# A decoder layer on one core: residual projection by tile, loads in program order, and a closing stage for one pair of experts

## The chip, the cores and the metric

The kernel runs on one core of one Trainium2 chip. A core has TensorE (PE), which multiplies matrices into an accumulator memory (PSUM) of eight banks, VectorE (DVE), ScalarE (ACT), GpSimd (POOL) and SyncE (SP), the engine that issues nearly all of this kernel's loads. Each engine works through its own list of instructions in order. An instruction that has to wait for another engine or for a DMA holds up all that is behind it on its own list. The metric is the device time of one execution in microseconds. The kernel before takes 1101.13 us (median of 3 runs, 1100.86 to 1102.59).

## The reference

One decoder layer on 512 tokens of width 1024, all in float32. The mixer's inner work is left out here; it is not touched.

```
y = hybrid_mixer(x, ...)                       # ends in a product with w_out (1024 x 1024)
x = layer_norm(DN_ALPHA * x + y, ln1_g, ln1_b)
y = memory_cross_attention(x, mem, x_wq, x_wkv, x_wo)
x = layer_norm(DN_ALPHA * x + y, ln2_g, ln2_b)
y = hier_moe(x, ...)
x = layer_norm(DN_ALPHA * x + y, ln3_g, ln3_b)

def memory_cross_attention(x, mem, wq, wkv, wo):   # 4 heads of 128, 256 memory tokens
    q = x @ wq;  k, v = split(mem @ wkv)
    p = softmax(q k^T / sqrt(128))
    return (p v) @ wo

def hier_moe(...):     # each token: the best of 4 groups, then the 2 best of its 8 experts
    gu = xc @ w_gu[e]                              # 1024 x 1024, e of 32 experts
    return (silu(gu[:, :512]) * gu[:, 512:]) @ w_down[e]   # 512 x 1024, times the token's weight, summed per token
```

## The kernel before, in words

The kernel has three stretches: the mixer, `mid` (L952 on: the residual projection with the first norm, then cross-attention with the second norm), and `moe` (L1894 on).

**Residual projection (L978 to L991).** The 512 tokens are four tiles q of 128 rows (`xt[q]`). The product of the mixer's output with `wout` is made in two halves ch of 512 columns. A half has four chunks kk of weights. Each chunk is loaded (`raw`, L220), split into a high and a low part (`wh` on ACT, L231, and `wl` on DVE, L232), and multiplied with all four tiles, so the four accumulators of a half are done at about the same time. `residual` (L878) then adds them to `xt[q]`. When the second half is in, the first norm of each tile follows (its square sum on ACT, the two passes of `norm_apply` on DVE), then eight transposes of the tile on PE (L1032) and their splits into `XH` and `XL` (L224, L225).

**Cross-attention.** K comes from `wk` and the memory (PSUM tile `s`, split into `kh` and `kl`), V from `wxv`. `project(f)` makes the queries of head f from `wq`. `score(f)` makes two PSUM tiles of scores (each half's row maximum on DVE, L1086, its product with -scale on DVE, L1087), the exponentials on ACT (L1092) and the division on DVE. `turn(f)` transposes the probabilities on PE and copies them to `PT` (the first half on ACT, L1111). `attend(f)` multiplies `PT` with V, `widen(k)` splits a chunk of `wxo`, and `out` multiplies with it.

**Experts.** The 32 experts are worked through in 16 pairs, p = 0 to 15. The weights of a pair are 12 units of 1 MB: 8 of the gate and up matrices (`gu`) and 4 of the down matrix (`dn`). Units are loaded in a fixed order into a ring of 24 homes (the ring proper and memory of earlier stages, so names such as `XL`, `raw` or `xt` stand for homes too). `load_first` (L1623) issues the first 24. `eat` (L1641) issues the next load into a home whose unit has been used. A pair takes eight steps `hidden(k)` into the two accumulators `pg`, then `activate` (SiLU on ACT, a product on DVE), `turn` (four transposes and a copy to `hT`), four `down_quarter` calls of 256 columns each, `scaled` (times the token's weight, split into `yh` and `yl`), and `combine`, which multiplies with the one-hot matrix `ohT` to add the pair's rows to the tokens, while the next pair's hidden steps run. The last two pairs are closed together by `finish` (L1724 to L1837): pair 14 stops after its transposes (L2005 to L2007). `finish` then mixes pair 15's hidden steps with the eight down quarters of both pairs, their scalings and eight products with `ohT` ("spills", L1746), four for each pair, and the third norm by 256 columns each, to write the last two tiles as four half rows (`ship`, L1708, with `idx2`). The last 16 loads stand in an order of their own (L1632, L1633). Tiles 0 and 1 have been written earlier (`settle`).

**What sets the order.** A list scheduler orders the instructions of the mixer and of `mid` up to L1051. From there all engines but SP keep the order in which the code is written. SP's list is ordered by the scheduler up to L1936 in `moe`, and only from there by the program.

Of the kernel before, what the change touches and what calls it, by code (L numbers as in the profile page):

```python
# [23 lines left out]
D = 1024  # L24
# [176 lines left out]
class K:  # L201
# [750 lines left out]
    def mid(self, outer, order):  # L952
# [13 lines left out]
        with ExitStack() as st:  # L966
# [12 lines left out]
            with ExitStack() as sw:  # L979
                pre = self.pool(sw, "pre", side="right")  # L980
                for ch in range(2):
                    acc = [self.t(ps, [128, 512], F32, "acc", 4) for _ in range(NT)]
                    for kk in range(4):
                        j = 4 * ch + kk
                        h, l = self.wsplit(a["wout"][j], wp=pre if 3 <= j < 7 else None)
                        for q in range(NT):
                            tk = slice(128 * q, 128 * q + 128)
                            self.mm3(acc[q], [(XH[:, 2 * kk + i, tk], XL[:, 2 * kk + i, tk], h[:, 512 * i:512 * i + 512],
                                               l[:, 512 * i:512 * i + 512]) for i in range(2)], start=kk == 0, stop=kk == 3)
                    for q in range(NT):  # L990
                        self.residual(stat[q], q, ch, acc[q], ALPHA)  # L991
# [57 lines left out]
            scale = 128.0 ** -0.5  # L1049
            ws = [self.wsplit(a["wq"][f]) for f in range(2)]  # L1050
# [22 lines left out]

            def score(f):
                qh, ql = qs[f]
                sm = self.t(mp, [128, 3, 4], F32, "sm", 2)
                tiles = []
                sps = []
                for b in range(2):
# [7 lines left out]
                    nc.vector.tensor_scalar(sm[:, 1, cs], sm[:, 0, cs], -scale, None, op0=ALU.mult)  # L1087
# [84 lines left out]
            score(3)  # L1172
            turn(2)
            widen(3, True)
# [133 lines left out]
    def route_init(self, mq, tri):  # L1308
# [17 lines left out]
        self.idx2 = self.t(rp, [128, NT, 2], I32, "idx2")  # L1326
# [47 lines left out]
    def use_records(self, mp, p, ps):  # L1374
# [18 lines left out]
        for i in range(2):  # L1393
            nc.vector.tensor_scalar(self.idx2[:, :, i], rec[:, :, 6], 2.0, float(i), op0=ALU.mult, op1=ALU.add)
# [228 lines left out]
    def load_first(self):  # L1623
# [36 lines left out]
    def activate(self, mp, pg, h=None):  # L1660
        if h is None:
            h, hT = self.halves(mp)
        else:
            hT = [self.t(self.m0, [128, 256], F32, f"oh{i}", 1) for i in range(2)]
        with self.tc.high_priority():
            self.nc.scalar.activation(h, pg[0], AF.Silu)  # L1666
            self.nc.vector.tensor_tensor(h, h, pg[1], op=ALU.mult)  # L1667
        return h, hT

    def turn(self, ps, h, hT):  # L1670
        pt = self.t(ps, [128, 512], F32, "t", 2)
        with self.tc.high_priority():
            for k in range(4):
                self.nc.tensor.transpose(pt[:, 128 * k:128 * k + 128], h[:, 128 * k:128 * k + 128], self.ident)  # L1674
            if isinstance(hT, list):
                for i, t in enumerate(hT):
                    self.nc.scalar.activation(t, pt[:, 256 * i:256 * i + 256], AF.Copy)
            else:
                self.nc.scalar.activation(hT, pt, AF.Copy)  # L1679
# [8 lines left out]
    def down_quarter(self, py, hT, p, c, experts, ks=range(4)):  # L1688
        us = [12 * p + 8 + 2 * (c // 2) + i for i in range(2)]
        for k in ks:  # L1690
            for i in experts:
                t = hT[k // 2][:, 128 * (k % 2):] if isinstance(hT, list) else hT[:, 128 * k:]
                self.mm(py[c][64 * i:64 * i + 64], t[:, 64 * i:64 * i + 64],
                        self.got[us[i]][c % 2][:, 256 * k:256 * k + 256], k == 0, k == 3)
        if k == 3 and c % 2:
# [12 lines left out]
    def ship(self, q, h=None):  # L1708
        o = self.views.pop()
        if h is None:  # L1710
            ix, z = self.idx[:, q:q + 1], self.xt[q]
        else:
            ix, o, z = self.idx2[:, q, h:h + 1], o.rearrange("t (h c) -> (t h) c", h=2), self.xt[q][:, 512 * h:512 * h + 512]
# [10 lines left out]
    def finish(self, mp, ps, last, hidden, turn):  # L1724
# [8 lines left out]
        def down(b, j, *experts, ks=range(4)):  # L1733
            if (b, j) not in py:
                py[b, j] = self.t(ps, [128, 512], F32, "ts"[j], 2)[:, :256]
            self.down_quarter({b: py[b, j]}, last[j][1], last[j][0], b, experts, ks)

        def scale(b, j):
            ws, o = last[j][3], y[b % 2][:, j]
            nc.scalar.activation(o[:, 0], py[b, j], AF.Copy, scale=ws)  # L1740
            nc.vector.scalar_tensor_tensor(o[:, 1], py[b, j], ws, f32(o[:, 0]), op0=ALU.mult, op1=ALU.subtract)

        def spill(b, j):
            for n, q in enumerate(span):
                if j == 0 and n == 0:
                    t = self.t(ps, [128, 512], F32, "acc", 4)  # L1746
                    acc[b, q], acc[b, q + 1] = t[:, :256], t[:, 256:]
                for i in range(2):
                    self.mm(acc[b, q], last[j][2][:, 128 * q:128 * q + 128], y[b % 2][:, j, i], j == 0 and i == 0 and n == 0, j == 1 and i == 1)

        def add(b):
            for q in span:
                z = self.xt[q][:, 256 * b:256 * b + 256]
                nc.vector.scalar_tensor_tensor(z, z, 1.0, acc[b, q], op0=ALU.mult, op1=ALU.add, accum_out=c(b, q))

        def square(b, qs=span):
            for q in qs:
# [9 lines left out]
        for k in range(4):  # L1767
            hidden(k)
        down(0, 0, 0, 1)
        scale(0, 0)  # L1770
        for k in range(4, NK):
            hidden(k)
        last.append(turn(lambda: spill(0, 0)))
        down(0, 1, 0, 1)
        scale(0, 1)
        down(1, 0, 0, 1)
        scale(1, 0)
        spill(0, 1)
        add(0)
        nc.vector.tensor_scalar(v(4), v(0), -4.0 / D ** 1.5, None, op0=ALU.mult)  # L1780
        down(1, 1, 0)
        spill(1, 0)
        down(1, 1, 1)
        scale(1, 1)
        square(0)
        down(2, 0, 0, 1)
        scale(2, 0)
        spill(1, 1)
        add(1)
        tt(9, 0, 1, ALU.add)  # L1790
        down(3, 0, 0, 1)
        scale(3, 0)
        spill(2, 0)
        square(1)
        down(2, 1, 0)
        spill(3, 0)
        down(2, 1, 1)
        scale(2, 1)
        down(3, 1, 0, 1, ks=(0, 1))
        spill(2, 1)  # L1800
        add(2)
        square(2)
        down(3, 1, 0, 1, ks=(2, 3))
        scale(3, 1)
# [4 lines left out]
        spill(3, 1)  # L1809
        add(3)  # L1810
        square(3)
        tt(5, 5, 7, ALU.add)
        stt(10, 3, -1.0 / D, 10, ALU.mult, ALU.add)
        stt(9, 3, -1.0 / D, 9, ALU.mult, ALU.add)
        stt(10, 10, -1.0, 10, ALU.mult, ALU.mult)
        halves = [(q, h) for q in span for h in range(2)]
        gb = self.gb3

        def centre(q, h):
            cs = slice(512 * h, 512 * h + 512)  # L1820
            z = self.xt[q][:, cs]
# [220 lines left out]
```

## Time and profile before

| | |
|---|---|
| median of 3 runs | 1101.13 us |
| profiled execution | 1106.79 us, of which the span of the instructions is 1105.2 us |
| TensorE | busy 1049.9 us, 95% of the span |
| VectorE / ScalarE / GpSimd | 49% / 37% / 11% |
| mean granted TensorE clock | 0.974 of full speed |
| moved by DMA | 266.61 MB, mean 241 GB/s over the span |

The second part of the page shows the span in 40 slices. The rate of the DMA is between 40 and 245 GB/s in the first half of the span and 413 to 421 GB/s in most slices from the 26th on, while PE is busy nine tenths of nearly every slice. A busy PE need not be one that computes at its full rate. A stretch table (windows) gives for a stretch each engine's busy time, the granted clock (1.00 is the full one), and the share of time in which the core's 16 DMA engines are busy.

### The profile page before, as it was taken

What the parts mean: (1) busy time and instruction counts of PE and PEld (TensorE: products, weight loads), DVE (VectorE), ACT (ScalarE), POOL (GpSimd) and SP (SyncE); (2) the same over time, 40 slices, a digit from 0 to 9 for tenths busy, and PEclk for the clock granted to TensorE, in tenths of its full rate; (3) what the DMA queues carried; (4) which work ended last, traced back from release to release, by engine and by line L of the source; (5) the groups of instructions that cost most, each with busy time, mean ns of one, the idle gap of its engine ahead of it and who ended that gap; (6) DMA issues with size and microseconds to landing.
All of it is one profiled execution on the core that took longest, in us unless ns stands there. A gap on an engine that the chain in (4) does not pass through costs nothing. (4 is left out here: it accounts for less than half of the span.)

```text
span 1105.2 us, 14593 instructions
## 1 busy us (share of the span) xinstructions
PE 1049.9 (95%) x5645; PEld 716.4 (65%) x5645; DVE 537.4 (49%) x1194; ACT 408.3 (37%) x763; POOL 117.0 (11%) x124
## 2 busy tenths in 40 slices
PE   7999999999999999998899999999999999999884
PEld 5688777778788778787768655465644565555342
DVE  6436656879956533646457444324341334322314
ACT  6325656557544422524356312031202122212112
POOL 1000002301311112326030000000000000000001
PEclk9999999999999999998999989999998999999987
DMA  6612123112322122666366879989999999999981
GB/s 244 233 63 77 58 70 120 40 58 96 105 77 79 55 95 82 245 241 236 126 235 240 334 304 386 413 360 414 419 420 403 394 421 419 419 421 419 419 371 39
DMA packets 52186, 266.61 MB, mean 241 GB/s; under 512 B 5905, under 2 KB 6193, under 8 KB 31505
## 3 DMA queue, kind: packets, MB, share of 16 engines
q1 hardware_dynamic: 49104, 255.18, 59.2%
q0 software_dynamic: 2432, 8.36, 2.0%
q10 hardware_dynamic: 576, 2.10, 0.6%
q8 instruction: 46, 0.75, 0.3%
q14 instruction: 28, 0.22, 0.1%
HBM read 261.42 MB, written 4.19 MB: 240 GB/s over the span
## 5 line engine op out<-in xcount | busy, mean ns | idle before, releaser
L240 PE MATMUL acc<-ring,xg 128*64 128x512 f32 x776 | 188.7, 600 | 7.1 <-DMA ring<-gu 6.3
L240 PEld LDWEIGHTS acc<-ring,xg 128*64 128x64 f32 x776 | 60.8, 138 | 107.2 <-issue 99.4
L232 DVE TENSOR_TENSOR wl<-raw,wh 128x1024 fp32r<-128x1024 f32 x63 | 78.1, 1242 | 79.1 <-PE mm L240 41.7
L240 PE MATMUL mm<-XH,wh 128*128 128x512 f32 x392 | 105.9, 399 | 6.6 <-ACT XH L224 5.1
L231 ACT ACTIVATE wh<-raw 128x1024 fp32r<-128x1024 f32 x71 | 75.1, 1059 | 94.3 <-PE mm L240 57.2
L240 PE MATMUL mm<-XL,wh 128*128 128x512 f32 x392 | 106.5, 397 | 0.0
L240 PE MATMUL mm<-XH,wl 128*128 128x512 f32 x392 | 105.9, 396 | 0.0
L240 PEld LDWEIGHTS mm<-XH,wh 128*128 128x128 f32 x392 | 73.0, 189 | 24.3 <-ACT XH L224 5.1
L240 PEld LDWEIGHTS mm<-XH,wl 128*128 128x128 f32 x392 | 73.3, 189 | 18.7 <-issue 3.8
L240 PEld LDWEIGHTS mm<-XL,wh 128*128 128x128 f32 x392 | 72.9, 189 | 15.9 <-issue 1.2
L1666 ACT ACTIVATE hh<-acc 128x512 f32<-128x512 f32 x15 | 9.0, 598 | 195.0 <-PE acc L240 182.1
L240 PE MATMUL t<-ring,hh 128*64 128x256 f32 x640 | 79.9, 381 | 0.7 <-ACT hh L1679 0.7
L1667 DVE TENSOR_TENSOR hh<-hh,acc 128x512 f32<-128x512 f32 x15 | 10.3, 688 | 139.6 <-PE acc L240 139.6
L1705 DVE SCALAR_TENSOR_TENSOR yl<-t,ws,yh 128x512 fp32r<-128x512 f32 x28 | 20.8, 750 | 107.6 <-ACT yh L1704 107.6
L240 PEld LDWEIGHTS t<-ring,hh 128*64 128x64 f32 x640 | 49.7, 137 | 23.5 <-ACT hh L1679 2.4
L856 POOL TENSOR_TENSOR mix<-mix,gate 128x512 f32<-128x512 f32 x24 | 37.6, 1571 | 191.2 <-DVE gate L855 173.5
L1565 ACT ACTIVATE xg<-acc,gbt 128x128 f32<-128x128 f32 x128 | 45.8, 477 | 21.8 <-PE acc L240 21.8
L240 PE MATMUL acc<-XL,xg 128*64 128x512 f32 x112 | 52.6, 620 | 1.2 <-DMA XL<-gu 1.2
L240 PE MATMUL s<-in,in 128*128 128x256 f32 (+5 forms) x198 | 43.8, 342 | 0.7 <-ACT S L630 0.7
L1704 ACT ACTIVATE yh<-t,ws 128x512 fp32r<-128x512 f32 x28 | 19.0, 687 | 66.8 <-PE t L240 52.4
L559 ACT ACTIVATE S<-S,sm 128x128 f32<-128x128 f32 (+3 forms) x48 | 26.7, 556 | 39.1 <-DVE sm L557 38.8
L240 PEld LDWEIGHTS s<-in,in 128*128 128x128 f32 (+1 forms) x198 | 33.3, 189 | 8.1 <-ACT S L630 0.9
(502 smaller groups left out, 1897.6 us busy)
## 6 DMA issues: line engine op xcount, KB each, us to landing
ring<-gu SPq DMA_DIRECT2D x95, 1024.0 KB, 13.5
ring<-dn SPq DMA_DIRECT2D x40, 1024.0 KB, 15.0
raw<-wing SPq DMA_DIRECT2D x32, 512.0 KB, 3.6
XL<-gu SPq DMA_DIRECT2D x14, 1024.0 KB, 12.5
ring<-gu SPq DMA_DIRECT2D x18, 512.0 KB, 13.0
XL<-dn SPq DMA_DIRECT2D x8, 1024.0 KB, 14.4
raw<-winf SPq DMA_DIRECT2D x15, 512.0 KB, 3.7
raw<-gu SPq DMA_DIRECT2D x13, 512.0 KB, 9.8
```

The source lines that it names most:

```text
L231: self.nc.scalar.activation(h, r, AF.Copy)
L232: (self.nc.gpsimd if pool else self.nc.vector).tensor_tensor(l, r, f32(h), op=ALU.subtract)
L240: self.nc.tensor.matmul(out, lhsT, rhs, start=start, stop=stop, skip_group_check=True)
L559: nc.scalar.activation(s[:, :n], s[:, :n], AF.Exp, bias=sm[:, 0, q:q + 1], scale=-1.0, accum_out=sm[:, 1, q:q + 1])
L856: nc.gpsimd.tensor_tensor(mix[d], mix[d], g, op=ALU.add)
L1565: self.nc.scalar.activation(t[:, d, :], p[:, d - 2 * b, w * k:w * k + w], AF.Identity, scale=self.gbt[:, d:d + 1], bias=self.gbt[:, NK + d ...
L1666: self.nc.scalar.activation(h, pg[0], AF.Silu)
L1667: self.nc.vector.tensor_tensor(h, h, pg[1], op=ALU.mult)
L1704: nc.scalar.activation(yh[:, cs], py[ch], AF.Copy, scale=ws)
L1705: nc.vector.scalar_tensor_tensor(yl[:, cs], py[ch], ws, f32(yh[:, cs]), op0=ALU.mult, op1=ALU.subtract)
```

## The change

1. **Residual projection by tile.** The second half of the columns has all its four chunks of weights split first and is then multiplied tile by tile; each tile's residual follows its own product.
2. **SP's list in program order from the loads of `wq` on.** The `manual_schedule` for SP is opened ahead of the first `wq` load in `mid` and no longer at `load_first`.
3. **Scores.** The product with -scale (L1087) becomes a Copy with a scale on ACT. For head 3, `score` is taken apart: its products, then `turn(2)` with its copy, then its exponentials.
4. **The last two pairs.** Pair 14 is closed as every other pair is, with its `combine` beside the hidden steps of pair 15 (two more `next(work)` at k = 3 and 5). `finish` closes pair 15 alone: four down quarters, four spills. The last 16 loads are in plain order. The last two tiles are written as two whole rows; `idx2` and its two DVE instructions go.

```diff
@@ mid
-                for ch in range(2):
-                    acc = [self.t(ps, [128, 512], F32, "acc", 4) for _ in range(NT)]
-                    for kk in range(4):
-                        j = 4 * ch + kk
-                        h, l = self.wsplit(a["wout"][j], wp=pre if 3 <= j < 7 else None)
-                        for q in range(NT):
...
-                    for q in range(NT):
-                        self.residual(stat[q], q, ch, acc[q], ALPHA)
...
+                w = [chunk(4 + kk) for kk in range(4)]
+                for q in range(NT):
+                    acc = self.t(ps, [128, 512], F32, "acc", 4)
                     for kk in range(4):
+                        product(acc, w[kk], kk, q)
+                    self.residual(stat[q], q, 1, acc, ALPHA)
...
             scale = 128.0 ** -0.5
+            order.enter_context(self.tc.manual_schedule(engines={nc.sync.engine}))
             ws = [self.wsplit(a["wq"][f]) for f in range(2)]
             order.enter_context(self.tc.manual_schedule(engines=self.engines))
@@ score
-                    nc.vector.tensor_scalar(sm[:, 1, cs], sm[:, 0, cs], -scale, None, op0=ALU.mult)
+                    nc.scalar.activation(sm[:, 1, cs], sm[:, 0, cs], AF.Copy, scale=-scale)
...
-            score(3)
+            products(3)
             turn(2)
+            soften(3)
@@ load_first
-        span = lambda x, y: list(range(n - x, n - y))
-        order = list(range(n - 16)) + span(12, 8) + span(16, 14) + span(8, 4) + span(4, 2) + span(14, 12) + span(2, 0)
-        self.in_ring = [j for j in order if j not in self.once and j not in self.again.values()]
+        self.in_ring = [j for j in range(n) if j not in self.once and j not in self.again.values()]
@@ moe
-        loads = ExitStack()
-        loads.enter_context(self.tc.manual_schedule(engines={nc.sync.engine}))
         self.load_first()
...
+                if p == n - 1 and k in (3, 5):
+                    next(work)
+                    next(work)
...
+            if p == n - 1:
+                self.finish(mp, ps, hT, p, ohT, ws)
+                break
...
-            if p == n - 2:
-                last, done = [(p, hT, ohT, ws)], None
-                continue
@@ finish (new order of its steps)
+        down(0)
+        scale(0)
+        down(1)
+        scale(1)
+        spill(0)
         add(0)
...
         square(0)
+        down(2)
+        spill(1)
+        scale(2)
         add(1)
+        square(1)
...
+        spill(2)
+        down(3)
         add(2)
+        scale(3)
         square(2)
...
+        spill(3)
         add(3)
         square(3)
...
         nc.gpsimd.tensor_tensor(v(11), v(5), self.mhalf.to_broadcast([128, 2]), op=ALU.pow)
+        centre(span[0], 1)
+        centre(span[1], 0)
+        for h in range(2):
+            apply(span[0], h)
+        self.ship(span[0])
+        centre(span[1], 1)
+        for h in range(2):
+            apply(span[1], h)
+        self.ship(span[1])
```

How the lists of the engines change at three places follows, first before, then now. A row is a line of the code, the operation, out<-in with the buffers' numbers, and the shape of what is moved or multiplied; x2 means two in a row.

PE in the second half of the residual projection, before: `acc_3978` to `acc_3981` are the accumulators of tiles 0 to 3, `wh_4044` the third chunk of weights.

```order
L240 MATMUL acc_3978<-wh_4044,XH_3780 128x512 x2
L240 MATMUL acc_3978<-wl_4045,XH_3780 128x512 x2
L240 MATMUL acc_3978<-wh_4044,XL_3781 128x512 x2
L240 MATMUL acc_3979<-wh_4044,XH_3780 128x512 x2
L240 MATMUL acc_3979<-wl_4045,XH_3780 128x512 x2
L240 MATMUL acc_3979<-wh_4044,XL_3781 128x512 x2
L240 MATMUL acc_3980<-wh_4044,XH_3780 128x512 x2
L240 MATMUL acc_3980<-wl_4045,XH_3780 128x512 x2
L240 MATMUL acc_3980<-wh_4044,XL_3781 128x512 x2
```

The same place now: `acc_4080` is tile 3's accumulator, `wh_3980` to `wh_3992` are chunks, and `xt_788` is tile 0.

```order
L240 MATMUL acc_4080<-wh_3980,XH_3780 128x512 x2
L240 MATMUL acc_4080<-wl_3981,XH_3780 128x512 x2
L240 MATMUL acc_4080<-wh_3980,XL_3781 128x512 x2
L240 MATMUL acc_4080<-wh_3986,XH_3780 128x512 x2
L240 MATMUL acc_4080<-wl_3987,XH_3780 128x512 x2
L240 MATMUL acc_4080<-wh_3986,XL_3781 128x512
L1042 MATMUL t_4346<-ident_58,xt_788_3805 128x128 x4
L1042 MATMUL t_4353<-ident_58,xt_788_3805 128x128 x4
L240 MATMUL acc_4080<-wh_3986,XL_3781 128x512
L240 MATMUL acc_4080<-wh_3992,XH_3780 128x512 x2
L240 MATMUL acc_4080<-wl_3993,XH_3780 128x512 x2
L240 MATMUL acc_4080<-wh_3992,XL_3781 128x512 x2
```

Before, each chunk went through all tiles and no tile was done until the last chunk. Now tile 3 takes its chunks one after another at the end, and the eight transposes of tile 0, whose norm lies behind its own product, stand amid tile 3's product.

SP ahead of the stream of expert weights, before: four loads into the ring stand ahead of these rows, and the other two `wq` and the `wxo` loads behind.

```order
L220 DMA raw_4261<-wxv 128x1024
L220 DMA raw_4279<-wxv 128x1024
L220 DMA raw_4297<-wxv 128x1024
L220 DMA raw_4315<-wxv 128x1024
L1609 DMA ring_1064_5332<-gu 128x2048
L1609 DMA ring_1065_5333<-gu 128x2048
L1609 DMA ring_1066_5334<-gu 128x2048
L1615 DMA ring_1063_5331<-gu 128x1024
L1615 DMA ring_4893<-gu 128x1024
L220 DMA raw_4484<-wq 128x1024
```

SP now, from the last `wxv` load on.

```order
L220 DMA raw_4315<-wxv 128x1024
L220 DMA raw_4485<-wq 128x1024
L220 DMA raw_4491<-wq 128x1024
L220 DMA raw_4526<-wq 128x1024
L220 DMA raw_4561<-wq 128x1024
L220 DMA raw_4626<-wxo 128x1024
L220 DMA raw_4628<-wxo 128x1024
L220 DMA raw_4630<-wxo 128x1024
L220 DMA raw_4681<-wxo 128x1024
L1628 DMA ring_1058_5328<-gu 128x2048
L1628 DMA ring_1059_5329<-gu 128x2048
```

The eight 1 MB units that stood among the loads of cross-attention (seven whole rows `ring<-gu` and one in two halves) now stand behind its last `wxo` load, and the `wq` loads stand right behind `wxv`.

SP at the end of the stream, before, from the first `gu` unit of pair 15 on (a unit is a row of 128x2048 or two of 128x1024; `dn` here is pair 14's).

```order
L1609 DMA ring_1065_5333<-gu 128x2048
L1609 DMA ring_1066_5334<-gu 128x2048
L1615 DMA ring_1063_5331<-gu 128x1024
L1615 DMA ring_4893<-gu 128x1024
L1609 DMA XL_4719<-gu 128x2048
L1609 DMA XL_4719<-dn 128x2048
L1615 DMA raw_4894<-dn 128x1024
L1615 DMA raw_4895<-dn 128x1024
L1609 DMA ring_1067_5335<-gu 128x2048
L1609 DMA ring_1068_5336<-gu 128x2048
```

The same places now.

```order
L1628 DMA ring_1064_5334<-dn 128x2048
L1628 DMA ring_1065_5335<-dn 128x2048
L1634 DMA ring_1062_5332<-dn 128x1024
L1634 DMA ring_4894<-dn 128x1024
L1628 DMA XL_4720<-dn 128x2048
L1628 DMA XL_4720<-gu 128x2048
L1634 DMA raw_4895<-gu 128x1024
L1634 DMA raw_4896<-gu 128x1024
L1628 DMA ring_1066_5336<-gu 128x2048
L1628 DMA ring_1067_5337<-gu 128x2048
```

Before, pair 15's `gu` units come first with two of pair 14's `dn` units between them, and pair 14's last two `dn` units come behind, among pair 15's. Now pair 14's four `dn` units come first, and pair 15's eight `gu` units follow.

## Rows read from the trace of the kernel before

**Rows 1.** The page: the span; busy time, share and instructions of TensorE.

```profile
span 1105.2 us, 14593 instructions
PE 1049.9 (95%) x5645; PEld 716.4 (65%) x5645; DVE 537.4 (49%) x1194; ACT 408.3 (37%) x763; POOL 117.0 (11%) x124
```

**Rows 2.** Stretches (start:end, length, busy us of PE, PEld, DVE, ACT, POOL, clock, DMA share, GB/s).

```profile
557.00:611.60 54.60, 51.45 (x291) 42.24 (x290) 38.60 (x158) 29.82 (x61) 11.69 (x12) 0.97 0.67 250
611.60:740.00 128.40, 123.34 (x777) 70.86 (x778) 46.09 (x132) 33.34 (x73) 3.94 (x4) 0.96 0.91 363
740.00:1074.50 334.50, 318.98 (x1912) 166.09 (x1908) 110.01 (x249) 65.14 (x142) 4.92 (x6) 0.98 1.01 415
1057.20:1066.60 9.40, 9.40 (x33) 2.71 (x33) 0.00 (x0) 0.60 (x1) 0.00 (x0) 0.74 1.01 420
```

**Rows 3.** Waits of SP, 620 to 740 us (total us, times, longest us).

```profile
SPq L1609 <- PE t L240: 38.0, 8, 14.2
```

**Rows 4.** Waits of PE, 500 to 531 us.

```profile
PE s L240 <- DVE kl L225: 3.9, 1, 3.9
PE acc L240 <- ACT wh L231: 3.0, 1, 3.0
PE t L1032 <- DVE XL L225: 1.1, 1, 1.1
```

**Rows 5.** Timeline of SP around cross-attention (start, duration, [idle before <-releaser]).

```profile
473.12 15.72 SPq L1609 DMA_DIRECT2D ring<-gu  x4
...
516.54 14.93 SPq L220 DMA_DIRECT2D raw<-wq  x4
...
558.08 0.38 SPq L220 DMA_DIRECT2D raw<-wxo  x1
```

**Rows 6.** Timeline of PE, then of ACT, around the K, V and query products.

```profile
500.60 1.11 PE L240 MATMUL s<-ol,wh 128*128 128x256 f32 x8
...
508.80 2.08 PE L240 MATMUL s<-oh,wh 128*128 128x256 f32 x8 [3.89 <-DVE kl L225]
...
529.91 3.52 PE L240 MATMUL acc<-XH,wh 128*128 128x512 f32 x8 [3.00 <-ACT wh L231]
...
535.12 1.98 PE L240 MATMUL acc<-XH,wl 128*128 128x512 f32 x8
...
528.80 2.17 ACT L231 ACTIVATE wh<-raw 128x1024 fp32r<-128x1024 f32 x2 [1.45 <-DMA raw<-wq]
```

**Rows 7.** Tile `xt` on DVE, 480 to 531 us (ns min/median/max); a row of POOL's timeline.

```profile
L915 DVE SCALAR_TENSOR_TENSOR xt<-xt,stat,ln x8: 737/744/2891, 491.3 to 507.7; 128x512 f32<-128x512 f32 x8
...
508.13 2.51 POOL L232 TENSOR_TENSOR wl<-raw,wh 128x1024 fp32r<-128x1024 f32 x1
```

**Rows 8.** Timeline, all engines, at the scores; then ACT at 622 us.

```profile
568.52 1.68 DVE L1087 TENSOR_SCALAR sm<-sm 128x2 f32<-128x2 f32 x1
...
571.86 1.12 PE L240 MATMUL acc<-PT,vm 128*128 128x512 f32 x2 [2.25 <-ACT PT L1111]
...
622.69 0.30 ACT L1480 ACTIVATE wsc<-wsc 128x4 f32<-128x4 f32 x1
```

**Rows 9.** Timeline of PE, the last two pairs.

```profile
1036.20 3.65 PE L240 MATMUL acc<-ring,xg 128*64 128x512 f32 x16 [1.52 <-DMA ring<-gu]
...
1057.14 9.51 PE L240 MATMUL acc<-ring,xg 128*64 128x512 f32 x32 [4.29 <-DMA ring<-gu]
...
1068.65 1.95 PE L240 MATMUL s<-ring,oh 128*64 128x256 f32 x16 [0.47 <-ACT oh L1677]
...
1072.25 0.74 PE L240 MATMUL acc<-yh,ohT 128*128 128x256 f32 x4
...
1090.52 1.14 PE L240 MATMUL acc<-yl,ohT 128*128 128x256 f32 x4 [1.05 <-ACT yl L1740]
```

**Rows 10.** Timeline of DVE, then of POOL, behind the last product.

```profile
1095.76 2.73 DVE L1827 SCALAR_TENSOR_TENSOR xt<-xt,stat,wl 128x512 f32<-128x512 f32 x4
...
1100.96 0.97 POOL L1714 DMA_INDIRECT out<-xt,idx  x1 [0.30 <-issue]
```

More of the change, by code (lines that the diff above doesn't have):

```diff
@@ L1072, in mid, with products @@
             probs = {}
+            raws = {}
             def score(f):
+                products(f)
+                soften(f)
+            def products(f):
                 qh, ql = qs[f]
                 sm = self.t(mp, [128, 3, 4], F32, "sm", 2)
-                tiles = []
                 sps = []
@@ L1658, in hidden, with activate @@
             self.eat(*us)
[L1660 to L1664, printed above, removed]
+    def activate(self, mp, pg):
+        h, hT = self.halves(mp)
         with self.tc.high_priority():
@@ L1674, in turn @@
                 self.nc.tensor.transpose(pt[:, 128 * k:128 * k + 128], h[:, 128 * k:128 * k + 128], self.ident)
[L1675 to L1679, printed above, removed]
+            self.nc.scalar.activation(hT, pt, AF.Copy)
     def down(self, ps, hT, p):
@@ L1686, in down, with down_quarter @@
         return py
[L1688 removed]
+    def down_quarter(self, py, hT, p, c, experts):
         us = [12 * p + 8 + 2 * (c // 2) + i for i in range(2)]
[L1690 removed]
+        for k in range(4):
             for i in experts:
[L1692 to L1693 removed]
+                self.mm(py[c][64 * i:64 * i + 64], hT[:, 128 * k + 64 * i:128 * k + 64 * i + 64],
                         self.got[us[i]][c % 2][:, 256 * k:256 * k + 256], k == 0, k == 3)
[L1695 removed]
+        if c % 2:
             self.eat(*[us[i] for i in experts])
@@ L1722, in settle, with finish @@
         self.ship(q)
-    def finish(self, mp, ps, last, hidden, turn):
+    def finish(self, mp, ps, hT, p, ohT, ws):
         nc = self.nc
@@ L1731, in finish, with down, scale, spill @@
         py, acc = {}, {}
[L1733 to L1743, printed above, removed]
-            for n, q in enumerate(span):
[L1745 to L1751, printed above, removed]
+        def down(b):
+            py[b] = self.t(ps, [128, 512], F32, "ts"[b % 2], 2)[:, :256]
+            self.down_quarter(py, hT, p, b, (1, 0))
+        def scale(b):
+            o = y[b % 2][:, b // 2]
+            nc.scalar.activation(o[:, 0], py[b], AF.Copy, scale=ws)
+            nc.vector.scalar_tensor_tensor(o[:, 1], py[b], ws, f32(o[:, 0]), op0=ALU.mult, op1=ALU.subtract)
+        def spill(b):
+            t = self.t(ps, [128, 512], F32, "acc", 4)
+            acc[b] = [t[:, 256 * n:256 * n + 256] for n in range(2)]
+            for i in range(2):
+                for n, q in enumerate(span):
+                    self.mm(acc[b][n], ohT[:, 128 * q:128 * q + 128], y[b % 2][:, b // 2, i], i == 0 and n == 0, i == 1)
+        def add(b):
+            for n, q in enumerate(span):
+                z = self.xt[q][:, 256 * b:256 * b + 256]
+                nc.vector.scalar_tensor_tensor(z, z, 1.0, acc[b][n], op0=ALU.mult, op1=ALU.add, accum_out=c(b, q))
+        def square(b):
             for q in span:
[L1753 to L1757, printed above, removed]
                 nc.scalar.activation(self.t(self.m0, [128, 512], F32, "wt", 2)[:, :256], self.xt[q][:, 256 * b:256 * b + 256], AF.Square,
```

102 lines of the change are left out of this document (30 added, 72 removed).

## The prediction

> **What bounds the kernel now.** I read the page first: TensorE is busy 1049.9 of 1105.2 us [rows 1]. The reader is to see that an average so high hides what sets the end. So the table of stretches came next [rows 2]. From 740 to 1074.5 us the DMA share is 1.01 at 415 GB/s: there the weight stream sets the pace, and a busy TensorE only keeps step. Before 740 it is the other way round: the share is 0.67 in 557 to 611.6 and 0.91 in 611.6 to 740. The queue's own waits show why. A full ring waits for TensorE, 38.0 us for the down products alone [rows 3]. Work that TensorE does earlier before 740 frees homes earlier, so the stream, and the end with it, can move forward by the same time. A few waits in front are what can be won there [rows 4]. Behind the stream stands a tail that TensorE sets again [rows 9]. The profiled execution took 1106.79 us, 5.7 more than the median 1101.13; I make the sum as a difference and take it off the median.
>
> **Projection, norm and load order.** In the K, V and query products TensorE waits 3.9 us for a split of K (`kl`), 3.0 for the first `wq` split, 1.1 for a split of a transposed tile: 8.0 together [rows 4]. Two of the groups behind a wait are also slow: 2.08 us against 1.11 for the same eight matmuls, 3.52 against 1.98 [rows 6], 2.5 more. That makes 10.5.
>
> The first and last waits have one cause. All four tiles' norms start together when the last chunk of `wout` is through, and DVE has K's splits queued among them. Now tiles 0 to 2 are normalised beside the products of the later tiles; the order of PE shows tile 0's transposes inside tile 3's product. Nothing is added: the same products, the same splits. The `wq` wait is the queue's. `wq` is issued at 516.54, behind the ring loads [rows 5], and ACT's first split starts at 528.80, after a wait for the DMA [rows 6]. Ahead of the ring, the `wq` loads go right behind `wxv`, and that wait goes. What is late next is tile 3: its residual and norm stand in DVE's order ahead of a `kl`, about one normal pass of 0.74 us and small steps [rows 7], which I put at 1.0. I take 10.5 - 1.0 = 9.5.
>
> The bounds: 10.5 if no new wait comes. At the other end only the `wq` wait and its slow group go, 3.0 + 1.5 = 4.5, since DVE's work is not less, only earlier.
>
> A row speaks against the full sum. The norm passes take 744 ns in the median but up to 2891, and POOL is busy with 2.51 us splits of weights in that stretch [rows 7]. The Trainium skill has the rule for this (SBUF — State Buffer, Who interferes with whom): a VectorE instruction with two inputs in SBUF contends with a GpSimd instruction that reads SBUF. By it, the norms' passes, with `xt` and the gains in SBUF, still meet POOL's splits wherever they are put; the 2.9 us passes agree with it. Two such meetings in front of a `kl` cost 2 x (2.89 - 0.74) = 4.3 and would leave 9.5 - 4.3 = 5.2, inside my bounds.
>
> **What the load order costs.** Eight units of 1 MB no longer start at 473 and before 516.54, but behind the last `wxo` load, at 558.08 before [rows 5] and, with the gain, near 548. At 415 GB/s a unit takes 1.049 MB / 415 = 2.53 us, eight take 20.2. The idle part of the DMA is 0.33 x 54.6 = 18.0 us in the first stretch and 0.09 x 128.4 = 11.6 in the second [rows 2], 29.6 in all. So the eight fit in before the stream binds. The ring's first 24 units then take 60.6 us, to about 608; pair 0 begins with units that have landed long before. I cost the move at nothing; if the cover is gone it costs up to 20.2.
>
> **Scores.** L1087 takes 1.68 us on DVE, beside a POOL split, where a small ACT operation takes 0.30 [rows 8]. Behind the exponentials of head 3, ACT copies `PT` late and TensorE waits 2.25 [rows 8]; now the copy stands ahead of them. I take 1.68 - 0.30 = 1.4. The best case is the whole 2.25. At worst all eight small operations land on ACT's path, 8 x 0.30 = 2.4 lost.
>
> **Closing.** Pair 14's last `gu` unit lands at 1036.2, since TensorE's wait for it ends there [rows 9]. Sixteen units follow; at 2.53 us each the last lands at 1076.7, before and now. All times in this part are without the shift from the front. Now: four `dn` units of pair 14 to 1046.3, eight `gu` units of pair 15 to 1066.6. Two hidden steps remain, a group of 16 as the one of 3.65 us: 1070.2. From the end of the hidden steps to the first quarter it was 1068.65 - (1057.14 + 9.51) = 2.0: 1072.2. Then four quarters of 1.95 and four spills of 0.74, 10.8. Two of the spills wait for a scaling, at 1.05 each by the last one [rows 9]: 1085.1. The last product ended at 1090.52 + 1.14 = 1091.7. The gain is 6.6. It comes from pair 14's quarters, which now run in the time in which TensorE waited for loads (4.29 us at 1057.14), and from four spills that become part of an ordinary `combine` there.
>
> Behind the last product, the first `apply` starts at 1095.76 and the fourth half-row write ends at 1101.9 [rows 10], 6.2 us later. Now five passes of 0.68, a gap of 0.30 and an issue of 0.97 make 4.7, though a row twice as long lands a little later: I take 1.1 (0 to 1.5). Closing together 6.6 + 1.1 = 7.7.
>
> The bound below: TensorE's granted clock was 0.74 in 1057.2 to 1066.6 [rows 2], after the 4.29 us wait, a mixture of the two levels of 1.2 and 2.4 GHz. There 32 matmuls took 9.51 us, where 16 took 3.65 (7.3 for 32). The new order waits for single landings before each pair of hidden steps, so the clock may be at the low level when the quarters start. The 10.8 us of quarters and spills would then take twice as long and the gain would be gone. The bound above is 10: no waits for scalings (2.1) and no slow start.
>
> **The sum.** 9.5 + 1.4 + 7.7 = 18.6 us less: 1088.2 against the profiled 1106.8, 1082.5 against the median. At the good ends it is 10.5 + 2.3 + 10 = 22.8 (1078.3), with two terms at poor values (4.5 and 0) 12.2 (1088.9). That is the likeliest case's own range, 1078 to 1089.
>
> **Rivals.**
> - *The front's gain is eaten by the late fill.* For: homes in memory of earlier stages come free late, so part of the DMA's idle time before 611.6 may not be usable for ring units, and the 20.2 us need two thirds of all the idle time. Against: the eight units go to ring homes that are free, and the stream waits on TensorE up to 740. If some 11 us of the move are not covered, only the closing is left: 1101.1 - 7.7 = 1093.4.
> - *The closing gains nothing.* For: the granted clock of 0.74 and single landings. Against: TensorE computes in each gap between landings. 1101.1 - 10.9 = 1090.2.
> - *Slower: the stream starts late and stays late.* Place: the ring's first fill. The stream now starts only when the last `wxo` buffer is free; if the splits ahead of that one are held by ACT or POOL, it starts at 558 as the `wxo` load did, TensorE's gain in front is lost at the first expert pairs, and all 20.2 us are paid: 1101.1 + 20.2 - 7.7 = 1113.6. It decides once less than 20.2 - 7.7 = 12.5 of the 29.6 us of idle DMA can be filled. Against it: nearly half of them would be enough.
> - *The change does not do what it says.* A manual order may leave PE waiting where the list scheduler had filled in. The orders show the intended moves, so this is only left as a residue: about 1101.
>
> **How the numbers follow.** Forecast 0.62 (1082.5); front eaten 0.15 (1093.4); closing without gain 0.13 (1090.2); slower 0.06 (1113.6); no change 0.04. Faster: 0.62 + 0.15 + 0.13 = 0.90; same 0.04; slower 0.06, with 0.2% (2.2 us) as about what a measurement of this kernel can tell. The range of 8 in 10 takes in the likeliest case's own range, the closing rival and most of the first: 1075 to 1094, its lower end some 3 us under the sum of the good ends, for waits that I did not see in one execution.
>
> **What would show it.** Right: no PE wait above 2 us for `kl` or for a `wq` split; the first project products some 9 us earlier; ring loads starting near 548; the DMA share over 0.9 from there to about 730 and 1.0 behind; no 4 us wait in pair 14 or 15 for a `gu` unit with work undone; the last product some 18 us behind the landing of the last `gu` unit, not 30 as before (1036.2 + 10 x 2.53 = 1061.5 against 1091.7). Wrong: a first landing of pair 0's or 1's units later than TensorE wants them (PE waits on DMA between 580 and 740), a clock near 0.5 in the last 20 us, or `kl` still waiting behind norm passes of 2 us and more.

## The result, and the profile after

The changed kernel takes 1083.97 us (median of 4 runs, 1083.70 to 1084.81) against 1100.99 us for the kernel before in the same runs: 17.0 us less, a ratio of 0.9844 with a 95% interval of 0.9811 to 0.9876. The forecast was 1082.5. The span of the profiled execution is 1082.2 us against 1105.2 [rows 1].

From the page of the changed kernel: its span, then busy time and share of each engine.

```profile
span 1082.2 us, 14565 instructions
...
PE 1037.9 (96%) x5637; PEld 709.1 (66%) x5637; DVE 532.2 (49%) x1186; ACT 408.5 (38%) x768; POOL 115.6 (11%) x122
```

The stretches that answer to [rows 2]. They begin 11 to 12 us earlier than there, and the last one ends 22.5 us earlier.

```profile
546.00:600.00 54.00, 52.36 (x311) 43.33 (x310) 36.93 (x162) 31.53 (x67) 12.57 (x12) 1.00 0.96 392
600.00:728.00 128.00, 122.90 (x767) 69.81 (x768) 45.31 (x125) 32.96 (x72) 3.94 (x4) 0.96 0.94 376
728.00:1052.00 324.00, 311.45 (x1894) 163.50 (x1890) 109.19 (x244) 63.19 (x137) 4.91 (x6) 0.99 1.01 417
```

The DMA share went from 0.67 to 0.96 in the first stretch and from 0.91 to 0.94 in the second. The stream itself runs at 417 GB/s, where it ran at 415. From 580 to 740 us PE waits for no load.

The front: PE's timeline, then SP's, answering to [rows 4 to 6].

```profile
501.25 1.21 PE L240 MATMUL s<-oh,wh 128*128 128x256 f32 x8 [1.45 <-DVE kl L225]
...
520.65 1.99 PE L240 MATMUL acc<-XH,wh 128*128 128x512 f32 x8
```

```profile
510.78 9.99 SPq L220 DMA_DIRECT2D raw<-wq  x4
523.68 24.23 SPq L220 DMA_DIRECT2D raw<-wxo  x4
547.95 3.58 SPq L1628 DMA_DIRECT2D ring<-gu  x7
```

The wait of 3.89 us for `kl` has become 1.45, the wait for `wq` is gone, and the queries' first group takes 1.99 us where it took 3.52. The ring's first loads go out at 547.95; the forecast said near 548.

The closing: PE's timeline, answering to [rows 9], then DVE and POOL behind the last product, answering to [rows 10].

```profile
1021.06 3.65 PE L240 MATMUL acc<-ring,xg 128*64 128x512 f32 x16 [1.05 <-DMA ring<-gu]
...
1042.41 3.65 PE L240 MATMUL acc<-ring,xg 128*64 128x512 f32 x16 [2.81 <-DMA ring<-gu]
...
1052.36 3.65 PE L240 MATMUL acc<-ring,xg 128*64 128x512 f32 x16 [0.19 <-DMA ring<-gu]
...
1058.22 1.95 PE L240 MATMUL t<-ring,hh 128*64 128x256 f32 x16 [0.69 <-ACT hh L1689]
...
1068.83 1.02 PE L240 MATMUL acc<-yl,ohT 128*128 128x256 f32 x4 [0.57 <-ACT yl L1744]
```

```profile
1073.34 1.41 DVE L1812 SCALAR_TENSOR_TENSOR xt<-xt,stat,wl 128x512 f32<-128x512 f32 x2
...
1077.26 0.98 POOL L1719 DMA_INDIRECT out<-xt,idx  x1 [0.96 <-DVE xt L1812]
```

Pair 14's last `gu` unit is used from 1021.06, pair 15's last from 1052.36, and the last product ends at 1069.85. Between landmarks on PE, in us, with a third profile of the kernel before that is told of below:

| from ... to | before | before, third | after | forecast gain |
|---|---|---|---|---|
| K's first product, queries' first product | 37.07 | 35.50 | 27.61 | 9.5 (with the next) |
| ... first transposes of P | 19.37 | 17.92 | 18.05 | |
| ... transposes of xt at the second norm | 36.95 | 36.99 | 34.31 | 1.4 |
| ... first `hidden` on a ring unit | 31.53 | 31.19 | 31.18 | 0 |
| ... wait for pair 14's last `gu` unit ends | 418.44 | 417.60 | 416.87 | 0 |
| ... last product ends | 55.46 | 55.89 | 48.79 | 6.6 |
| ... end of the span | 13.54 | 13.46 | 12.35 | 1.1 |

The sum over the first profile is 23.2 us, over the third 19.4; by the medians the gain is 17.0.

### The profile page after: what moved, and what is told of

Same layout as the page of the kernel before. It is cut to its first block, busy times and chain, and to the rows that moved or that the text cites. A ratio compares the mean times of both kernels' runs of the same rounds, so it can differ in the third digit from the quotient of the medians.

```text
span 1082.2 us, 14565 instructions
## 1 busy us (share of the span) xinstructions
PE 1037.9 (96%) x5637; PEld 709.1 (66%) x5637; DVE 532.2 (49%) x1186; ACT 408.5 (38%) x768; POOL 115.6 (11%) x122
## 5 line engine op out<-in xcount | busy, mean ns | idle before, releaser
L240 PE MATMUL acc<-ring,xg 128*64 128x512 f32 x768 | 182.7, 593 | 5.0 <-DMA ring<-gu 4.2
L240 PE MATMUL t<-ring,hh 128*64 128x256 f32 x688 | 86.4, 381 | 2.1 <-ACT hh L1689 2.1
L240 PEld LDWEIGHTS t<-ring,hh 128*64 128x64 f32 x688 | 53.5, 137 | 26.3 <-ACT hh L1689 4.2
L559 ACT ACTIVATE S<-S,sm 128x128 f32<-128x128 f32 (+3 forms) x48 | 26.6, 555 | 39.1 <-DVE sm L557 38.8
```

The costliest lines, as they stand in the source:

```text
L240: self.nc.tensor.matmul(out, lhsT, rhs, start=start, stop=stop, skip_group_check=True)
L559: nc.scalar.activation(s[:, :n], s[:, :n], AF.Exp, bias=sm[:, 0, q:q + 1], scale=-1.0, accum_out=sm[:, 1, q:q + 1])
```

## Experiments

**The kernel before, twice more.** No edit. The first expectation is that of the second profile.

> The kernel before, unchanged, for a second profile of it: the first profiled execution took 1106.8 us, 5.7 over the median. Theory: those 5.7 us are an accident of one execution (its granted clock was 0.974), so a second profile is near 1101 us, the waits of 3.9 (kl), 3.0 (wq) and 2.25 us (PT) are there again, the product of head 0's queries starts some 9 us later than in the changed kernel (520.6), and the expert stage some 13 us later. Rival: the front's waits themselves vary from run to run; then one of them is missing in the second profile, and the terms of the sum were read from an unusual execution.

Measured: 1101.19 us (median of 12; 1096.50 to 1105.80); profiled execution 1105.80 at clock 0.974. All three front waits are there again (3.9 us for `kl`, 2.8 for the first `wq` split, 2.3 for `PT`), and the queries begin 36.8 us behind K.

> The kernel before once more, for a third profile. Its executions lie between 1096 and 1106 us and the time falls as the mean granted clock rises (0.984 at 1096.5, 0.974 at 1105.8); both profiles so far show 0.974. Theory (how long the clock stays low behind TensorE's waits differs from one execution to the next, and the profiles caught long ones): if this profile's clock is over 0.978, it lacks one of the slow stretches at 500 to 550 us or behind 1050 us, and its time is about 1 us lower per 0.001. Rival (the profiler itself costs the kernel before some 5 us): 0.974 and 1105 to 1107 us a third time.

Measured: 1100.68 us (median of 10), profiled execution 1102.37 at clock 0.977. First the second profile, then the third: the queries' first group on PE, and the stretches at 525 to 550 and 600 to 625 us.

```profile
528.67 3.58 PE L240 MATMUL acc<-XH,wh 128*128 128x512 f32 x8 [2.79 <-ACT wh L231]
...
525.00:550.00 25.00, 22.21 (x106) 18.51 (x106) 10.66 (x20) 9.20 (x18) 0.00 (x0) 0.93 0.36 123
600.00:625.00 25.00, 23.25 (x143) 16.30 (x143) 18.08 (x94) 13.13 (x28) 1.65 (x2) 0.93 0.74 267
```

```profile
527.65 2.11 PE L240 MATMUL acc<-XH,wh 128*128 128x512 f32 x8 [1.44 <-ACT wh L231]
...
525.00:550.00 25.00, 23.56 (x121) 19.85 (x120) 12.74 (x26) 10.62 (x25) 0.00 (x0) 1.00 0.35 122
600.00:625.00 25.00, 22.50 (x142) 13.73 (x143) 15.54 (x76) 12.07 (x27) 1.66 (x2) 1.00 0.69 239
```

The waits for `kl` (3.9 us) and `PT` (2.3) are the same in all three profiles. The wait for the first `wq` split is not: 3.00 us in the first profile [rows 6], 2.79 in the second, 1.44 in the third, where ACT did not have to wait for the load. Behind the shorter wait the clock is 1.00 and not 0.93, and the first group takes 2.11 us and not 3.58. So for this one wait the rival of the second profile holds: it varies from one execution to the next. At 600 to 625 us PE stands no less than in the second profile (busy 22.50 us against 23.25), and the clock is 1.00 against 0.93 all the same. The execution is 3.4 us shorter. The clock as a whole was only 0.977, a little under the 0.978 that the expectation named, but one of the slow stretches that it named is missing. Two of the three waits belong to the kernel; the size of the third, and how long the clock stays low, belong to the execution. Over 69 executions of the kernel before the time went from 1096.5 us at 0.984 to 1109.2 at 0.973, on a straight fit 0.95 us for 0.001. So the first profile, at 0.974 and 5.7 us over the median, stood at the slow end, and that is in the main why its sum (23.2) exceeds the medians' difference.

**Projection by chunk.**

```diff
-                w = [chunk(4 + kk) for kk in range(4)]
-                for q in range(NT):
-                    acc = self.t(ps, [128, 512], F32, "acc", 4)
-                    for kk in range(4):
-                        product(acc, w[kk], kk, q)
-                    self.residual(stat[q], q, 1, acc, ALPHA)
...
+                for ch in range(2):
+                    acc = [self.t(ps, [128, 512], F32, "acc", 4) for _ in range(NT)]
+                    for kk in range(4):
...
+                    for q in range(NT):
+                        self.residual(stat[q], q, ch, acc[q], ALPHA)
```

> The changed kernel with the residual projection by chunk as before; load order, scores and closing as changed. Theory (norms beside the product remove K's waits, 3.9 + 1.1 + 1.0 less 1.5 that remained): a kl wait of some 4 us is back, 4 to 6 us slower than the changed kernel, 1088 to 1090 us. Rival (the waits moved behind POOL's weight splits anyway, and the load order alone made the gain): within 1.5 us of the changed kernel, 1084 to 1085.5.

Measured: 1090.69 us (ratio to before 0.9893, 0.9869 to 0.9916), 6.7 us slower than the changed kernel by the medians, a little more than expected. Its waits of PE from 470 us on:

```profile
PE s L240 <- DVE kl L225: 6.0, 1, 6.0
...
PE t L1032 <- DVE XL L225: 1.1, 1, 1.1
```

The `kl` wait is 6.0 us, longer than the 3.9 before. DVE and POOL just ahead of it, first of this kernel, then of the kernel before:

```profile
503.55 4.98 DVE L916 SCALAR_TENSOR_TENSOR xt<-xt,stat,ln 128x512 f32<-128x512 f32 x2
502.75 5.24 POOL L232 TENSOR_TENSOR wl<-raw,wh 128x1024 fp32r<-128x1024 f32 x2
```

```profile
504.12 2.91 DVE L916 SCALAR_TENSOR_TENSOR xt<-xt,stat,ln 128x512 f32<-128x512 f32 x2
503.31 2.50 POOL L232 TENSOR_TENSOR wl<-raw,wh 128x1024 fp32r<-128x1024 f32 x1
```

Two passes of a norm take 4.98 us beside two splits of weights on POOL, where they took 2.91 beside one. That is 2.1 us more, and the wait is longer by as much. The queries begin 36.6 us behind K, and 27.6 with the tiles: 9.0 us of the front are the tile order's. Without the tile order the new load order hardly shows: from K's first product to the first transposes of P it takes 54.6 us here, and 56.4, 56.2 and 53.4 in the three profiles of the kernel before.

**Ring loads early again.**

```diff
-            order.enter_context(self.tc.manual_schedule(engines={nc.sync.engine}))
             ws = [self.wsplit(a["wq"][f]) for f in range(2)]
...
+        loads = ExitStack()
+        loads.enter_context(self.tc.manual_schedule(engines={nc.sync.engine}))
```

The lines that come in stand ahead of `load_first`, where they stood in the kernel before; where `loads` is closed again is left out.

> The changed kernel with the loads ordered by the scheduler up to the expert stage as before, so that eight ring units go out ahead of wxv's end, wq and wxo. Theory (the wq wait and its slow matmuls come back, 3.0 + 1.5, and an early start of the stream is worth nothing): 3 to 6 us slower than the changed kernel, 1087 to 1090 us, with a wait of TensorE for wq's split above 2 us. Rival (a late start of the stream costs part of its 20 us): the stream is earlier here, the expert stage has fewer waits, and the time is the same or lower, 1078 to 1084.

Measured: 1084.58 us (0.9849, 0.9820 to 0.9877). Neither theory holds as it stood. The time is that of the changed kernel, as the rival said, but waits of PE did come back, for `wxv` and not for `wq`:

```profile
PE s L240 <- ACT wh L231: 2.0, 2, 1.2
...
PE s L240 <- POOL wl L232: 1.2, 1, 1.2
```

From K's first product to the first transposes of P it takes 49.6 us, 45.7 in the changed kernel. What made up for them lies elsewhere. The clock at 60 to 100 us, first of the changed kernel, then of this one:

```profile
60.00:80.00 20.00, 20.00 (x111) 17.16 (x110) 4.47 (x12) 2.55 (x4) 0.00 (x0) 0.96 0.24 79
80.00:100.00 20.00, 20.00 (x84) 15.97 (x84) 13.34 (x35) 11.12 (x27) 0.00 (x0) 0.87 0.21 71
```

```profile
60.00:80.00 20.00, 20.00 (x115) 16.99 (x114) 5.13 (x13) 2.55 (x4) 0.00 (x0) 1.00 0.25 79
80.00:100.00 20.00, 20.00 (x98) 16.03 (x97) 12.90 (x34) 13.07 (x31) 0.00 (x0) 1.00 0.24 79
```

PE is busy throughout in both, and does 98 matmuls where it did 84. K's first product starts 3.3 us earlier (489.77 against 493.04), in a stretch that the edit does not touch. Why the clock stays up there stays open. In the other profiles, whose edits do not touch that stretch either, the clock at 80 to 100 us is 0.84 to 0.93, and K's first product starts between 491.7 and 494.6 us. So the load order is worth 4.0 us where it acts, and 0.6 in the time of the kernel by the medians, which these runs do not separate from none. The start of the stream, 78 us earlier for its first four units (469.55), brought nothing.

**The old closing on the new front, and the new closing on the old front.**

```diff
+            if p == n - 2:
+                last, done = [(p, hT, ohT, ws)], None
+                continue
...
```

The rest of this edit is left out: `finish`, the order of the last 16 loads and the half rows are those of the kernel before. The second kernel is the kernel before with part 4 of the change alone.

> The kernel before with projection, load order and scores changed, but its old closing of two pairs, old order of the last 16 loads and four half-row writes. Theory (closing worth 7.7, front 10.9): 1084 + 7.7 = 1091.7, between 1089 and 1094, with a wait of some 4 us for a gu unit while pair 14's down products are still to be done. Rival (the closing gains nothing of its own; the whole gain of 17 us is from the front): 1083 to 1086.

Measured: 1090.76 us (0.9898, 0.9873 to 0.9922), 6.8 us slower than the changed kernel. PE's timeline has the wait with pair 14's down products still to be done:

```profile
1042.81 3.68 PE L240 MATMUL acc<-ring,xg 128*64 128x512 f32 x8 [4.27 <-DMA ring<-gu]
```

From the end of the wait for pair 14's last `gu` unit it takes 56.2 us to the last product (48.8 in the changed kernel) and 13.4 behind it.

> The kernel before with the new closing alone (pair 14 as a normal pair, plain order of the last 16 loads, two whole-row writes); projection, SP's order and scores as before. Theory (the closing's gain does not depend on the front): some 7 us faster than before, 1092 to 1096 us, with 49 us from the first matmul that waits for pair 14's last gu unit to the last product (55.5 before) and 12.4 behind it (13.5 before). Rival (it gains only together with the earlier front): under 3 us.

Measured: 1094.44 us (0.9938, 0.9916 to 0.9959), 7.3 us under the 1101.75 of before in those runs. The same two lengths are 48.8 us and 12.3 us. The closing's gain does not hang on the front.

**How much later may the stream start?** Extra copies of 1 MB from the weights to a spare place in DRAM, ahead of the first ring load: four in the first kernel (shown), eight in the second.

```diff
...
+        for j in range(4):
+            self.nc.sync.dma_start(self.spare[j], self.src[20 + j])
         for j in self.in_ring[:len(self.homes)]:
```

> The changed kernel with four copies of 1 MB from the expert weights to a spare place in DRAM put on SP's queue ahead of the first ring load (extra work; outputs unchanged). The DMA idles 0.04 x 54 + 0.06 x 128 = 9.8 us between 546 and 728 us in the changed kernel. Theory (the late start is covered by that idle time): four copies of at least 2.5 us, 10 us, cost 0 to 3 us: 1084 to 1087. Rival A (the start is not covered at all): 10 us or more, 1094 and up. Rival B (the stream does not matter there): 0, and 0 for eight as well.

> The same with eight copies, at least 20 us. Theory: the idle 9.8 us are used up and the rest is paid: 10 to 13 us slower than the changed kernel, 1094 to 1097, with DMA share 1.0 from 548 us on. Rival A: 20 us and more, 1104 and up. Rival B: 1084 to 1085.

Measured: 1094.94 us (0.9938, 0.9912 to 0.9963) with four and 1107.51 (1.0045, 1.0025 to 1.0065) with eight: 11 and 23.5 us more. The theory fell; rival A's numbers came. But the place is not a wait for weights. PE's longest wait from 570 to 740 us, first with four copies, then with eight:

```profile
PE s L240 <- ACT zT L1229: 8.7, 2, 8.4
```

```profile
PE s L240 <- ACT zT L1229: 22.6, 2, 22.3
```

With four copies, ACT's timeline shows what held `zT` up; SP's row is the load that released it.

```profile
580.73 1.24 ACT L1239 ACTIVATE xt<-xt,stat 128x1024 f32<-128x1024 f32 x1
592.12 0.34 ACTq L1240 DMA_DIRECT2D zd<-xt  x1
592.51 1.06 ACT L1241 ACTIVATE wh<-xt 128x1024 fp32r<-128x1024 f32 x1 [10.54 <-DMA raw<-gu]
593.48 1.07 ACT L1229 ACTIVATE zT<-t 128x512 f32<-128x512 f32 x2
```

```profile
575.87 2.82 SPq L1635 DMA_DIRECT2D raw<-gu  x2
```

ACT stands for 10.5 us ahead of its store of the normalised tile (`zd`). Each DMA of this program counts its completion on a semaphore, a counter that others can wait for. In the trace this store uses semaphore 115, and the DMA that used it last is the first `raw<-gu` load, a unit for which the store has no use. SP's loads and ACT's stores share eight such counters, and POOL's DMAs count on others. That load was issued at 575.87 and landed at about 592.1. In the changed kernel the same load is issued at 562.41 and takes 16.2 us, so it lands at 578.6; the store goes out at 581.29. The room was 2.7 us. The copies put the load 13.5 us later, and 13.5 less 2.7 is 10.8: what ACT stood (10.5) and what the kernel lost (11).

**The same copies, with the store on POOL.**

```diff
-                nc.scalar.dma_start(self.zd[128 * q:128 * q + 128, :], z)
+                nc.gpsimd.dma_start(self.zd[128 * q:128 * q + 128, :], z)
```

> The four copies again, and the four stores zd<-xt issued by POOL and not by ACT. In the run with the copies ACT stood 10.5 us ahead of its first zd<-xt store, until a raw<-gu load had landed that store has nothing to do with: both use the same one of eight completion counters, so the store cannot be issued before the load is done. Theory (this wait of ACT's, and not a weight that came too late, is what made the late start cost 11 us): without it the four copies cost 0 to 4 us, 1084 to 1088, and the 8.4 us wait of TensorE for zT is gone. Rival (the stream itself is too late): 1093 to 1096, with waits of TensorE for ring loads of pair 0 or 1 in place of the one for zT.

Measured: 1083.58 us (0.9852, 0.9830 to 0.9874): the four copies now cost nothing. The store on POOL without the copies was not run; but from K's first product to the first `hidden` on a ring unit it takes 111.2 us here as in the changed kernel, so up to there no gain of the store hides a cost of the copies. The longest waits of PE from 570 to 740 us, and the two stretches:

```profile
PE acc L240 <- DVE oh L1542: 1.6, 2, 0.8
PE t L240 <- ACT hh L1692: 1.4, 2, 0.7
```

```profile
546.00:600.00 54.00, 52.19 (x313) 43.17 (x311) 37.35 (x169) 31.05 (x65) 13.64 (x16) 1.00 0.98 387
600.00:728.00 128.00, 123.04 (x770) 68.78 (x772) 46.23 (x122) 32.98 (x72) 3.89 (x4) 0.97 1.02 416
```

The second stretch shows a share of 1.02: the idle time of the DMA there could be used after all, once ACT did not have to wait for the stream.

**K in four PSUM buffers.**

```diff
-                p = self.t(ps, [128, 512], F32, "s", 2)
+                p = self.t(ps, [128, 512], F32, "acc", 4)
```

> The changed kernel with K's four products in the PSUM buffers of tag acc (four) and not of tag s (two), so that the third product need not wait for kl of the first, which stands behind a norm pass of tile 3 on DVE (1.45 us). Theory: that wait goes, the queries' product starts 1.0 to 1.5 us earlier after K's first product (26.1 to 26.6 us, 27.6 now), 1082.5 to 1083.2 us. Rival (another wait takes its place, for an accumulator that tile 3's residual still holds, or for kl later): 27.4 us or more and 1083.7 to 1085.

Measured: 1082.77 us (0.9838, 0.9813 to 0.9863). The `kl` wait is gone; one of 0.7 us for a tile's split is left, and the queries begin 26.6 us behind K, 1.0 earlier. The kernel's median is the lowest measured, 1.2 us under the changed kernel's, a difference that these runs do not separate from none.

**The scores, one half at a time.** The stretch meant here is that from the first transposes of P to those of `xt`: 36.95 us before, 34.3 in the changed kernel.

```diff
-                    nc.scalar.activation(sm[:, 1, cs], sm[:, 0, cs], AF.Copy, scale=-scale)
+                    nc.vector.tensor_scalar(sm[:, 1, cs], sm[:, 0, cs], -scale, None, op0=ALU.mult)
```

> The changed kernel with the product with -scale back on DVE; the order products, turn, exponentials stays. From the first transposes of P to those of xt it takes 36.95 us before and 34.3 now. Theory (the copy ahead of the exponentials alone removes the 2.25 us wait): 34.3 to 34.6. Rival (the 1.68 us operation beside POOL's split was the cause): 35.5 to 36.5, with a wait for PT or for the scores. Time 1083.5 to 1086 either way.

Measured: 1084.14 us; the stretch takes 35.1 us, and PE's timeline has

```profile
560.51 1.12 PE L240 MATMUL acc<-PT,vm 128*128 128x512 f32 x2 [0.43 <-DVE PT L1134]
```

```diff
-            products(3)
-            turn(2)
-            soften(3)
+            score(3)
+            turn(2)
```

> The changed kernel with score(3) whole again ahead of turn(2); the product with -scale stays on ACT. Theory (the order removed the wait): a wait of TensorE for PT of 1 to 2.3 us is back and the stretch takes 35.3 to 36.6 us. Rival (the operation on DVE was the cause): no such wait, 34.3 to 34.6.

Measured: 1085.45 us; the stretch takes 35.2 us, and PE's timeline has

```profile
559.36 2.22 PE L240 MATMUL acc<-PT,vm 128*128 128x512 f32 x4 [0.36 <-ACT PT L1132]
```

Neither half is the cause alone. Each by itself takes the wait for `PT` from 2.25 us to 0.4 and some 1.8 of the 2.65 us away; the second adds 0.8.

## Why the prediction was right

**Projection and norm.** Right in kind; the size depends on the profile. The two first lines of the table give 10.8 us for the first profile and 7.8 for the third, where 9.5 were forecast. The `wq` wait was only in part the queue's: of its 3.00 us in the first profile ACT waited 1.45 for the load [rows 6], and in the third, with no wait for the load, 1.44 are still there, because ACT's copies of V (`vm`) stand ahead of the split. In the changed kernel ACT's list has the split first:

```profile
518.10 1.06 ACT L231 ACTIVATE wh<-raw 128x1024 fp32r<-128x1024 f32 x1 [2.41 <-PE s L240]
519.91 0.60 ACT L1029 ACTIVATE vm<-s 128x512 f32<-128x512 f32 x1 [0.75 <-PE s L240]
```

The wait left over is at the place named, `kl` behind tile 3's norm, and 1.45 us, not 1.0. DVE and POOL of the changed kernel show why:

```profile
497.50 3.36 DVE L915 SCALAR_TENSOR_TENSOR xt<-xt,stat,ln 128x512 f32<-128x512 f32 x2
500.78 0.41 DVE L225 TENSOR_TENSOR kl<-s,kh 128x256 fp32r<-128x256 f32 x1
```

```profile
494.90 4.75 POOL L232 TENSOR_TENSOR wl<-raw,wh 128x1024 fp32r<-128x1024 f32 x2 [3.52 <-ACT wh L231]
```

Two passes that take 1.4 us alone take 3.36 while POOL splits a weight. This is what the rule cited from the Trainium skill (SBUF — State Buffer, Who interferes with whom) says, and the rows agree. It cost far less than the 4.3 us weighed in the prediction, because only one meeting stands ahead of a `kl` that PE needs. In the kernel by chunk the passes met two splits on end, and PE waited 6.0 us for `kl`.

**The split between tile order and load order** was off. Taking the tile order out costs 6.7 of the 17 us, where the prediction's terms for it come to 5.0. The load order saves 4.0 us where it acts, near the 4.5 that I had for it, but only 0.6 in the kernel's time in these runs; the trace shows a higher clock at 60 to 100 us in the run without it. And the two do not simply add: without the tile order, the load order's gain is in the main taken back by a longer `kl` wait.

**Scores.** Mis-sized: 2.65 us where 1.4 was taken and 2.25 given as the best. The step that failed is "1.68 - 0.30 = 1.4" as the value of both edits. They act on one chain (maximum, product with -scale, exponentials, copy of `PT`), and the measurement shows that each removes most of the wait and both together all of it and a little more.

**Late start of the stream.** The result, no cost, was right. The reason given was not. I counted 29.6 us of idle DMA against 20.2 and took the remaining 9.4 as room. The four copies show that the room was 2.7 us, and that an average share does not give it: the first deadline in the stretch is what counts. The "slower" rival had the right place, the first fill, but I said of it that nearly half of the idle time would be enough. That it did not come is in part luck: three microseconds later it would have begun to come true, by a way that I had not named, an ACT store that waits for a load with which it shares a counter.

**Closing.** Right in each step. Pair 14's last `gu` unit is 15.1 us earlier; with these 15.1 us added to the measured times, the forecast ones against them are 1066.6 against 1067.5 for pair 15's last `gu` unit, 1072.2 against 1073.4 for the first quarter, 1085.1 against 1085.0 for the last product. The quarters start 1.2 us late, and the two waits for scalings are 0.24 and 0.57 us where 1.05 each were taken; these two errors offset each other. The tail shrank by 1.2 us where 1.1 was forecast. Removing it or adding it alone moved the time by 6.8 and 7.3 us. The rival with a low clock in the quarters did not come: they take 1.95 us each.

**The base.** Making the sum as a difference and taking it off the median was what kept the forecast close. But 3.0 of the 10.5 us counted in front belong to the first profile and not to the kernel: in the third, the `wq` wait is 1.6 us shorter and the group behind it 1.4. Held against the third profile, the front gave 1.7 us less than forecast, the scores 1.3 more and the closing 0.5 more. So part of the closeness of the total (1082.5 against 1083.97) is luck.

## What to carry to other kernels

A mean idle share of the DMA over a stretch does not say how much later a stream may start. Look for the first instruction on any engine that waits for one of its loads, and count shared completion counters among the things waited for, since an engine's store can wait for an unrelated load ahead of it. When tiles become ready one by one, what follows them on other engines can be hidden under the products of the later tiles; that was worth 6.7 us here, about as much as the closing. The price of a wait read from one profile can hold a longer wait, or a stretch of low clock, that other executions lack: profile the kernel more than once before pricing it.

## What the runs showed of the hardware that was not expected

A store issued by ACT stood 10.5 us for a load on SP's queue whose data it does not use; issued by POOL it did not wait, and four copies of 1 MB went from costing 11 us to costing nothing. The granted clock of whole executions of one unchanged kernel ranged from 0.973 to 0.984, and the time with it from 1109.2 to 1096.5 us. At 80 to 100 us, which no edit touches and in which PE is busy throughout, the clock was 0.84 to 1.00 in the profiles of this record.
